# A weight sum tied behind splits of activations, and one head's outputs stored in two parts

## The chip, the cores and the metric

The kernel runs on one core of one Trainium2 chip. The metric is the time of one execution on the device in microseconds, as the median of several runs.

## The reference

The computation is one inference step of a two-layer trunk for 512 sample tokens and 128 prompt tokens, 2048 channels, float32. Each layer takes an RMS norm with shift and scale from a conditioning vector, one wide input projection whose columns feed two mixers and their gates, one output projection, and a gated residual. The second layer's first mixer is differential attention with four heads. Cut to that and to what follows it:

```python
cq, ck, cv, cg, dq, dk, dv, dg = split_cols(h @ w_in, ODD_SPLIT)
...
o1 = attend(cq[:, 0][:, :, None], ck_all[:, 0], cv_all)[:, :, 0]
o2 = attend(cq[:, 1][:, :, None], ck_all[:, 1], cv_all)[:, :, 0]
o_c = rms_norm(o1 - lam.astype(o1.dtype) * o2, c_on) * (1.0 - lam_init)
y_c = o_c.transpose(0, 2, 1, 3).reshape(b, t, C_W) * jax.nn.silu(cg)
y_d = merge_heads(attend(q_d, dk_all, dv_all)) * jax.nn.silu(dg)
return jnp.concatenate([y_c, y_d], axis=-1) @ w_out, new
...
xp = xp + gt_p * out_p
xs = xs + gt_s * out_s
```

`x_prompt` and `x_sample` give the two groups of tokens; both go through the same weights.

## The kernel before

All 640 tokens lie side by side on the free axis: columns 0 to 511 are the sample, 512 to 639 (`SPLIT`) the prompt; a half is 320 columns (`HALF`, `HV`). Channels lie on the 128 partitions, so an activation of 2048 channels is 16 tiles `h0` to `h15`. Matrix products keep float32 accuracy by splitting each operand into a high and a low part: ScalarE copies the high part (`split`, line 328), VectorE subtracts it (line 329), and TensorE makes three products (lines 364 to 366, and 667 to 669 in pairs of tiles). Weights come in quarters of 256 KB (`load_raw`, line 341, tile `raw`, four buffers) or in halves of 512 KB (`load8`, line 582, tile `w8`, shown as `w`, four buffers).

The instructions of each engine run in a fixed order. That order is not the order of the code: the framework plans it before the run from its own estimates of durations, taking what it thinks is ready first, and earlier code before later code among that. An engine that waits for an instruction's input holds everything behind it. The same holds for the loads that SyncE (SP) issues and the stores that GpSimd (POOL) issues.

**The last output projection** (`project`, `project_out`, called with layer 1) takes the 16 output tiles in three kinds. Tiles 0 to 3 and the first steps of the next work run while the last attention ends. Tiles 4 and 5 are made singly; the last single tile, 5, makes all its second halves of columns first (PSUM `pb`) and then the first halves (`pa`). From tile 6 on, tiles come in pairs by seven half-sized products M1 to M7 in place of eight (Strassen's scheme with Winograd's sums, `run_pairs`). For that, sums and differences of the activations' quarters are needed:

- `forms` makes them during the single tiles, for j = 0 to 7 from the tiles j and j + 8: three forms x2, x3, x4 in a tile `x` (lines 1284 to 1286), which is split into the tiles `T`, and a difference `d` = b12 - b11 (line 1287), kept unsplit in `t1[j]`. The inputs `ya`, `yb` come from DRAM into two `w8` buffers. `x` lies in the tile `sx` (one buffer). `d` lies in the free places `tables` for j < 4, in `sf` for j = 4 to 6, and for j = 7 over b11 itself in its `w8` buffer.
- When tile 5 has read the second halves of h0 to h7, `project` writes the split differences over them (lines 328 and 329, `h<-tables`, `h<-sf`, `h<-w`). They are the moving operand of M5.
- `run_pairs` loads the weight blocks A11, A21, A22 (two quarters in `raw`) and A12. The operand of M5 is the sum A21 + A22, made in two instructions (line 606) in a tile `sx`, the same buffer as the forms' x. M6 and M3 change that sum in place (lines 609, 618); line 611 makes another difference in `sf`. All these are split before use. M1 takes A11 as it is.

Results of a tile are added to the residual (`res_sum`, line 1304, tile `xr`), turned by TensorE (line 697), copied and stored (`rows_out`). A fill of VectorE work (lines 211 and 213, weights of the modulation in `adaw` and `tables`, loaded by POOL, line 218) runs beside it.

**The differential heads** (`diff_gen`) work in units of 128 query tokens: units 0 to 3 are the sample, 4 the prompt. Unit u is scored in step u (lines 927 to 929, maxima in line 889, exponentials in line 896), weighed two steps later (lines 1733 to 1738, a norm with POOL's lines 1743 and 1744 and VectorE's line 1748), and turned and written to `y` by `out` another step later (lines 1753 to 1758). Heads 0, 1 and 3 have their gates ready, and `out` multiplies with them. The third head, h = 2, has none (`gt is None`); its two output tiles y4 and y5 are copied by ScalarE (line 1756) and stored by POOL to DRAM (`save_y`, line 1050, `ydram`). Their gates are the last two tiles of the input projection (columns `cg` 4 and 5, `last_gate`, `very_late_gate`): the head's output is loaded again (line 1413, tile `yg`), the gate is made from PSUM (lines 1415 and 1416), the product (line 1419, tile `gg`) goes to DRAM (line 1420), and `y1_maker` (line 2046) loads it for the output projection.

Of the kernel before, what the change touches and what calls it, by code (L numbers as in the profile page):

```python
# [23 lines left out]
NS = 512  # L24
NP = 128
NT = NS + NP
HALF = NT // 2
# [5 lines left out]
SPLIT = slice(NS, NT)  # L33
# [21 lines left out]
def trunk_kernel(ctx: ExitStack, tc: tile.TileContext, I: dict, O: dict):  # L55
    nc = tc.nc
    V, A, PE, G = nc.vector, nc.scalar, nc.tensor, nc.gpsimd
# [31 lines left out]
    def psT():  # L89
        return pT.tile([P, 512], F32, tag="T", name="T")  # L90
# [236 lines left out]
    def split(hi, lo, x):  # L327
        A.activation(hi, x, AF.Copy)  # L328
        V.tensor_sub(lo, x, hi)  # L329
# [46 lines left out]
    prep, attn = [], []  # L376
# [12 lines left out]
    late = []  # L389
# [648 lines left out]
    ydram = [dram.tile([P, NT], F32, name=f"yd{k}") for k in range(KT)]  # L1038
# [6 lines left out]
    y = [None] * KT  # L1045
    st = {"sets": 1, "rp": 3}

    def save_y(*ks):
        for k in ks:
            nc.gpsimd.dma_start(ydram[k], y[k])  # L1050
# [198 lines left out]
    def big(tag, shape=(P, NT), dtype=F32, bufs=1):  # L1249

        n = 6 * HALF if tag[0] == "T" else 8 * P
        return pools["cur"].tile([P, n], dtype, tag=tag, name=tag, bufs=bufs)

    def forms(src):

        f = None

        kept = isinstance(src, dict)

        def load(j):  # L1260
            if kept:
                return src[j], src[j + 8]
            if src is None:
                for k, n in ((j, "acc"), (j + 8, "sq")):
                    V.tensor_add(st[n], *hs[k])
                return st["acc"], st["sq"]
            ts = [big("w8", bufs=4)[:, 0:NT] for _ in range(2)]
            for i in range(2):
                nc.sync.dma_start(ts[i], src[j + 8 * i])
            return ts  # L1270

        T.clear()
        t1.clear()
        nxt = load(0) if src and not kept else None
        for j in range(8):
            (ya, yb), nxt = nxt or load(j), (load(j + 1) if src and not kept and j < 7 else None)
            b11, b12, b21, b22 = ya[:, 0:HALF], ya[:, HALF:NT], yb[:, 0:HALF], yb[:, HALF:NT]
            x = big("sx")[:, 0:3 * HALF]
            if f is None:
                f = big("sf")  # L1280
            d = (room[j] if j < 4 else f[:, (j - 4) * HALF:(j - 3) * HALF] if j < 7
                 else big("w8", bufs=4)[:, 0:HALF] if kept else b11)
            x2, x3, x4 = (x[:, i * HALF:(i + 1) * HALF] for i in range(3))
            V.tensor_sub(x3, b22, b12)
            V.tensor_add(x2, b11, x3)
            V.tensor_sub(x4, b21, x2)
            V.tensor_sub(d, b12, b11)
            t = big(f"T{FORM_AT[j] if kept else j}", dtype=F32R).rearrange("p (s n) -> p s n", s=2)
            split(t[:, 0, :], t[:, 1, :], x)
            T.append(t)  # L1290
            t1.append(d)
            yield
# [113 lines left out]
        project(W_OUT[l], [n * P for n in range(KT)], n0, maker, job, begin, done, tail, **kw)  # L1406


    def very_late_gate(i, places):
        def f(pp):  # L1410
            ap = pools["cur"]
            ti, t, g = (ap.tile([P, NT], F32, tag=tag, name=n, bufs=b) for n, (tag, b) in zip(("yg", "gt_t", "gg"), places))
            nc.sync.dma_start(ti, ydram[i])
            for j, sl in HV:
                A.activation(t[:, sl], pp[j][:, 0:HALF], AF.Tanh, scale=0.5)
                V.scalar_tensor_tensor(out=g[:, sl], in0=t[:, sl], scalar=1.0, in1=pp[j][:, 0:HALF],
                                       op0=ALU.add, op1=ALU.mult)
            yield
            V.tensor_mul(g, ti, g)
            nc.gpsimd.dma_start(ydram[i], g)  # L1420
        return f

# [269 lines left out]
    def diff_gen(ap, h, v, kq):  # L1692

        gt = gates_back(2 * h)
        t = y_pair(2 * h) if gt is None else gt
        ps, pts, ons, rls, fins, rns = {}, {}, {}, {}, {}, {}

        maps = []

        def score(u, m):  # L1700
            segs, masks, lo, hi, _ = blk_plan(u, False)
            n = hi - lo
            k, q = kq[m]
            s = scores(q, u, k, segs)
            maps.append(soft(ap, 768, s[:, lo:hi], n, q[2][u]))
            if m == 0:
                return
            pp, ll, _ = zip(*maps)
            maps.clear()
            ps[u] = pp[0]  # L1710

            def mix():
                rr = [inverse(l) for l in ll]
                w = small.tile([P, 1], F32, tag="w", name="w")
                V.scalar_tensor_tensor(out=w, in0=ll[0], scalar=nlam, in1=rr[1], op0=ALU.mult, op1=ALU.mult)
                V.scalar_tensor_tensor(out=pp[0][:, 0:n], in0=pp[1][:, 0:n], scalar=w, in1=pp[0][:, 0:n],
                                       op0=ALU.mult, op1=ALU.add)
                rls[u] = rr[0]
            fins[u] = later_on(mix)

        def groups(u):
            n = len(blk_plan(u, False)[4])
            fins.pop(u)()
            pts[u] = [pt_group(ap, [ps[u][:, i * P:(i + 1) * P] for i in range(c0, min(c0 + 4, n))])
                      for c0 in range(0, n, 4)]

        def weigh(u):
            chunks = blk_plan(u, False)[4]
            last = len(chunks) - 1
            o = psT()[:, 0:256]  # L1730
            pieces = [(i, c, [x[:, (i % 4) * P:(i % 4) * P + P] for x in pts[u][i // 4]]) for i, c in enumerate(chunks)]
            for i, c, (ph, _) in pieces:
                PE.matmul(o, ph, v[0][:, c, :], start=(i == 0), stop=False)
                PE.matmul(o, ph, v[1][:, c, :], start=False, stop=False)
            for i, c, (_, pl) in pieces:
                PE.matmul(o, pl, v[0][:, c, :], start=False, stop=(i == last))
            on = ap.tile([P, 256], F32, tag="on", name="on", bufs=2)
            A.activation(on, o, AF.Copy, scale=rls[u])
            both = small.tile([P, 2], F32, tag="ssq", name="ssq")
            ssq, rns[u] = both[:, 0:1], both[:, 1:2]  # L1740
            junk = ap.tile([P, 256], BF16, tag="junk", name="junk")
            A.activation(junk, on, AF.Square, accum_out=ssq)
            G.tensor_scalar(ssq, ssq, 1.0 / 256, EPS, ALU.mult, ALU.add)
            G.tensor_tensor(rns[u], ssq, half[:, 0:1], op=ALU.pow)
            ons[u] = on

        def norm(u):
            V.scalar_tensor_tensor(out=ons[u], in0=ons[u], scalar=rns[u], in1=st["con"], op0=ALU.mult, op1=ALU.mult)

        def out(u):  # L1750
            x = psT()
            for j in range(2):
                PE.transpose(x[:, j * P:(j + 1) * P], ons[u][:, j * P:(j + 1) * P], ident)
            d, x = t[:, :, u * P:(u + 1) * P], x[:, 0:256].rearrange("p (j q) -> p j q", j=2)
            if gt is None:
                A.copy(d, x)
            else:
                V.tensor_mul(d, x, d)

        yield  # L1760
        for u in range(8):
            if u >= 3:
                out(u - 3)
            if 2 <= u < 7:
                weigh(u - 2)
            if u < 5:
                score(u, 0)
            if u == 7:
                break
            yield  # L1770
            if u >= 2:
                norm(u - 2)
            if u < 5:
                score(u, 1)
            if u == 4:
                passed["scores"] += 1
            if u == 6:
                passed["values"] += 1
            if 1 <= u < 6:
                groups(u - 1)  # L1780
            yield
        save_y(2 * h, 2 * h + 1)
        passed["heads"] += 1


# [162 lines left out]
    def gates_back(i):  # L1948
        if i not in FRONT:
            return None  # L1950
        t = y_pair(i)
        for j in range(2):
            nc.sync.dma_start(t[:, j, :], gdram[i + j])
        return t
# [65 lines left out]
        jobs.append((OD["cq"] + h * P, q_job("q0", "c_q_norm", keep=("x2", 1))))  # L2020
        jobs.append((OD["cq"] + (4 + h) * P, with_rest("q1", "c_q_norm", head_rest, h, done0 + 4 + h)))
    def last_gate(i):
        late = very_late_gate(i, (("rp", 3), ("stg", 2), ("rp", 3)))

        def f(pp):
            wait_for("heads", 3)
            return late(pp)
        return f
# [20 lines left out]
    def last_pool():  # L2049
        close("odd")  # L2050
        close_psum("twice")
        open_psum("more")
        open_pool("fin")
        for n in range(2):
            res_load(1, n)
        attn.append(forms(ydram))

    def rows_out(n):
        xr = st["xr", n]
# [94 lines left out]
```

## Time and profile before

| | us |
|---|---|
| median of three runs | 2225.78 |
| the three runs | 2224.23, 2225.78, 2227.52 |
| the profiled execution | 2222.26 |
| its span, first to last instruction | 2220.5 |
| busy in it: TensorE matmuls | 2189.8 |
| VectorE | 1741.9 |
| ScalarE | 1128.7 |
| GpSimd | 251.5 |

Rows of a timeline give the start from the beginning of the span and the duration in microseconds, engine, line, operation, out<-in with shapes, and how often; a bracket gives how long the engine stood idle before it and what ended that. "SPq" is SyncE's queue of loads. Rows of waits give the sum, the number and the longest. Rows of transfers give their number, the size of one in KB and the median time from issue to landing.

### The profile page before, as it was taken

Reading aid. Unit: us, or ns where it says so; the run is one execution under the profiler, and the core shown is the slowest. Engines: PE = TensorE matmul, PEld = TensorE weight load, DVE = VectorE, ACT = ScalarE, POOL = GpSimd, SP = SyncE. Lnnn points to the kernel's source line nnn. Section 1 sums busy time; section 2 is a strip of 40 time slices with the busy share of each in tenths; the row PEclk is TensorE's granted clock in tenths of the full one; section 3 lists DMA queues with packets and bytes.
Section 4 is the critical chain, followed back from the end, with each engine's and each line's share of the span. In section 5 each row is a group of like instructions: output and inputs, shape, how many; then the busy total and the mean of one; then the engine's idle time right before and its main releaser. Section 6 shows DMA issues by size and latency. Waiting matters only on the chain.

```text
span 2220.5 us, 40890 instructions
## 1 busy us (share of the span) xinstructions
PE 2189.8 (99%) x15456; PEld 2121.2 (96%) x15456; DVE 1741.9 (78%) x3047; ACT 1128.7 (51%) x2405; POOL 251.5 (11%) x401
## 2 busy tenths in 40 slices
PE   7999999999999999999999999999999999999999
PEld 5899999999999999999999999999999999989998
DVE  5669898989888977877888878978667666677775
ACT  4335453535334445444644466554577766663343
POOL 3220000000100100000101012211010011111110
PEclk9999999999999999999999999999999999999999
DMA  9986556565554435844554434545523233347641
GB/s 367 336 295 185 174 160 207 178 199 159 158 151 123 146 100 185 248 137 125 168 153 142 145 98 128 167 140 163 176 81 97 68 115 112 117 128 256 194 141 52
DMA packets 377172, 359.26 MB, mean 162 GB/s; under 512 B 18562, under 2 KB 326240, under 8 KB 376464
## 3 DMA queue, kind: packets, MB, share of 16 engines
q1 hardware_dynamic: 354944, 279.54, 41.6%
q0 software_dynamic: 21168, 74.90, 9.6%
q8 instruction: 121, 1.98, 0.4%
q10 hardware_dynamic: 864, 2.23, 0.3%
q14 instruction: 75, 0.61, 0.1%
HBM read 307.17 MB, written 44.17 MB: 158 GB/s over the span
## 4 chain that ended last, share of the span: by engine, by line
PE 90%; DMA 4%; DVE 3%; issue 2%; ACT 1%; POOL 0%; SPq 0%; DVEq 0%; POOLq 0%; ACTq 0%
PE pq L667 13%; PE pq L669 12%; PE pq L668 12%; PE pa L364 6%; PE pa L365 6%; PE pb L364 6%; PE pa L366 6%; PE pb L366 6%; PE pb L365 6%; PE T L915 2%; PE S L927 1%; PE S L928 1%; PE T L195 1%; PE S L929 1%; PE T L978 1%
## 5 line engine op out<-in xcount | busy, mean ns | idle before, releaser
L328 ACT ACTIVATE wh<-raw 128x512 fp32r<-128x512 f32 (+1 forms) x352 | 210.5, 600 | 316.2 <-PE pb L365 194.0
L667 PE MATMUL pq<-h,wh 128*128 128x320 f32 x1152 | 359.0, 312 | 0.0
L669 PE MATMUL pq<-h,wl 128*128 128x320 f32 x1152 | 356.5, 309 | 0.0
L668 PE MATMUL pq<-h,wh 128*128 128x320 f32 x1152 | 356.4, 309 | 0.0
L364 PE MATMUL pa<-h,wh 128*128 128x320 f32 x944 | 299.2, 317 | 1.0 <-ACT h L328 1.0
L364 PE MATMUL pb<-h,wh 128*128 128x320 f32 x944 | 295.9, 314 | 0.0
L365 PE MATMUL pa<-h,wh 128*128 128x320 f32 x944 | 294.5, 312 | 0.0
L366 PE MATMUL pb<-h,wl 128*128 128x320 f32 x944 | 294.1, 312 | 0.0
L365 PE MATMUL pb<-h,wh 128*128 128x320 f32 x944 | 293.7, 311 | 0.0
L366 PE MATMUL pa<-h,wl 128*128 128x320 f32 x944 | 292.9, 310 | 0.0
L329 DVE TENSOR_TENSOR wl<-raw,wh 128x512 fp32r<-128x512 f32 (+1 forms) x352 | 228.7, 650 | 76.4 <-ACT wh L328 72.1
L667 PE MATMUL pq<-T,wh 128*128 128x320 f32 x864 | 269.0, 311 | 0.4 <-DVE tables L646 0.4
L669 PE MATMUL pq<-T,wl 128*128 128x320 f32 x864 | 267.3, 309 | 0.4 <-DVE wl L329 0.4
L668 PE MATMUL pq<-T,wh 128*128 128x320 f32 x864 | 267.2, 309 | 0.0
L328 ACT ACTIVATE wh<-sx 128x512 fp32r<-128x512 f32 x216 | 135.7, 632 | 181.9 <-PE pq L668 111.9
L667 PEld LDWEIGHTS pq<-h,wh 128*128 128x128 f32 x1152 | 216.4, 188 | 2.1 <-issue 2.1
L668 PEld LDWEIGHTS pq<-h,wh 128*128 128x128 f32 x1152 | 216.5, 188 | 0.0
L669 PEld LDWEIGHTS pq<-h,wl 128*128 128x128 f32 x1152 | 216.3, 188 | 0.0
L282 DVE SCALAR_TENSOR_TENSOR acc<-adaw,sT,acc 128x1024 f32<-128x1024 f32 x150 | 189.2, 1277 | 0.0
L364 PEld LDWEIGHTS pa<-h,wh 128*128 128x128 f32 x944 | 177.3, 188 | 11.1 <-issue 8.7
L365 PEld LDWEIGHTS pa<-h,wh 128*128 128x128 f32 x944 | 177.6, 188 | 5.0 <-issue 4.7
L329 DVE TENSOR_TENSOR wl<-sx,wh 128x512 fp32r<-128x512 f32 x216 | 147.8, 688 | 43.4 <-ACT wh L328 39.7
(438 smaller groups left out, 4949.6 us busy)
## 6 DMA issues: line engine op xcount, KB each, us to landing
adaw<-in_ada_w SPq DMA_DIRECT2D x80, 512.0 KB, 4.2
raw<-in_ev_w_in SPq DMA_DIRECT2D x130, 256.0 KB, 3.6
raw<-in_od_w_in SPq DMA_DIRECT2D x112, 256.0 KB, 3.0
w<-in_od_w_in SPq DMA_DIRECT2D x48, 512.0 KB, 4.2
ada<-in_ada_w SPq DMA_DIRECT2D x11, 2048.0 KB, 13.1
adaw<-in_ada_w POOLq DMA_DIRECT2D x69, 256.0 KB, 3.6
w<-in_ev_w_in SPq DMA_DIRECT2D x27, 512.0 KB, 3.8
adah<-in_ada_w SPq DMA_DIRECT2D x20, 512.0 KB, 9.0
```

The lines of the kernel that those rows point to most:

```text
L195: PE.matmul(acc[32 * g:32 * g + 32, 0:wd], sT[:, kt, :], w[:, kt % m, :], start=(i < 4), stop=(i >= KT - 4), tile_position=(0, 32 * g))
L282: V.scalar_tensor_tensor(out=acc[c], in0=w, scalar=sT[:, kt, c:c + 1], in1=acc[c], op0=ALU.mult, op1=ALU.add)
L328: A.activation(hi, x, AF.Copy)
L329: V.tensor_sub(lo, x, hi)
L364: PE.matmul(ps, wh[:, i, :], hi[:, sl], start=(j == js[0] if alone else (pos == 0 and j == 0)), stop=False)
L365: PE.matmul(ps, wh[:, i, :], lo[:, sl], start=False, stop=False)
L366: PE.matmul(ps, wl[:, i, :], hi[:, sl], start=False, stop=(j == js[1] - 1 if alone else (pos == 3 and j == 3)))
L667: PE.matmul(ps, wh[:, j, :], hi, start=(first and h == 0 and j == 0), stop=False, skip_group_check=True)
L668: PE.matmul(ps, wh[:, j, :], lo, start=False, stop=False, skip_group_check=True)
L669: PE.matmul(ps, wl[:, j, :], hi, start=False, stop=(final and h == 1 and j == 3), skip_group_check=True)
L915: PE.transpose(t[:, i * P:(i + 1) * P], p, ident)
L927: PE.matmul(d, q[0][:, bs], k[0][:, ks], start=True, stop=False)
```

## The change

Two independent edits.

In the forms of the last projection alone (`hold`), for j = 7: the tile `x` with the forms lies in a `w8` buffer instead of `sx`, and the difference `d` lies in `sx` instead of over b11. The tile `sx` is thus held until that difference has been split over h7, and the sums of line 606, which need the same buffer, come after that split.

For the third differential head: instead of two stores of 640 columns behind the last unit, there are two stores of the 512 sample columns after unit 3 is written (step 6) and two of the 128 prompt columns after unit 4 (step 7). The two late gates of these tiles load the two parts separately and multiply them separately; the product is stored in one piece as before.

```diff
-    def forms(src):
+    def forms(src, hold=False):
...
-            x = big("sx")[:, 0:3 * HALF]
+            x = (big("w8", bufs=4) if hold and j == 7 else big("sx"))[:, 0:3 * HALF]
             if f is None:
                 f = big("sf")
             d = (room[j] if j < 4 else f[:, (j - 4) * HALF:(j - 3) * HALF] if j < 7
-                 else big("w8", bufs=4)[:, 0:HALF] if kept else b11)
+                 else big("sx")[:, 0:HALF] if hold else big("w8", bufs=4)[:, 0:HALF] if kept else b11)
...
-    def very_late_gate(i, places):
+    def very_late_gate(i, places, parts=(slice(0, NT),)):
...
-            nc.sync.dma_start(ti, ydram[i])
+            for sl in parts:
+                nc.sync.dma_start(ti[:, sl], ydram[i][:, sl])
...
-            V.tensor_mul(g, ti, g)
+            for sl in parts:
+                V.tensor_mul(g[:, sl], ti[:, sl], g[:, sl])
             nc.gpsimd.dma_start(ydram[i], g)
...
             if u >= 3:
                 out(u - 3)
+            if gt is None and u >= 6:
+                for k in (2 * h, 2 * h + 1):
+                    sl = SPLIT if u == 7 else slice(0, NS)
+                    nc.gpsimd.dma_start(ydram[k][:, sl], y[k][:, sl])
...
-        save_y(2 * h, 2 * h + 1)
+        if gt is not None:
+            save_y(2 * h, 2 * h + 1)
...
-        late = very_late_gate(i, (("rp", 3), ("stg", 2), ("rp", 3)))
+        late = very_late_gate(i, (("rp", 3), ("stg", 2), ("rp", 3)), (slice(0, NS), SPLIT))
...
-        attn.append(forms(ydram))
+        attn.append(forms(ydram, True))
```

## Prediction

> **What bounds the kernel now.** The page first: TensorE is busy all but 30.7 us of the span, so only time in which TensorE stands or runs slowly can be won.
>
> ```profile
> span 2220.5 us, 40890 instructions
> PE 2189.8 (99%) x15456; PEld 2121.2 (96%) x15456; DVE 1741.9 (78%) x3047; ACT 1128.7 (51%) x2405; POOL 251.5 (11%) x401
> ```
>
> The profiled execution took 2222.26 us, 1.76 more than its span; the median of the three runs is 2225.78, which is 3.52 above the profiled one. I work out a difference on the profiled run and take it off the median. A measurement of this kernel can tell about 0.2%, 4.45 us, from no change.
>
> Then the waits of TensorE over the whole span, longest first. The first belongs to the start of the kernel; the next two lie where the change acts.
>
> ```profile
> PE T L1078 <- DMA xb<-in_x_sample: 6.5, 2, 5.1
> PE T L697 <- issue: 2.8, 1, 2.8
> PE S L927 <- ACT p L896: 2.4, 1, 2.4
> ```
>
> **The place of the tie.** Four stretches around the second of these waits (columns: length, busy time of PE, PEld, DVE, ACT and POOL, then granted clock, DMA share, GB/s):
>
> ```profile
> 2065.00:2069.00 4.00, 3.87 (x25) 3.34 (x23) 1.30 (x2) 3.73 (x9) 0.00 (x0) 1.00 0.22 64
> 2069.00:2072.00 3.00, 0.33 (x3) 0.26 (x3) 2.19 (x5) 0.41 (x1) 0.00 (x0) 1.00 0.08 24
> 2072.00:2076.00 4.00, 4.00 (x18) 3.88 (x18) 4.00 (x11) 0.75 (x2) 1.35 (x3) 0.57 0.72 216
> 2076.00:2080.00 4.00, 4.00 (x30) 4.00 (x29) 3.00 (x4) 0.63 (x1) 0.47 (x1) 1.00 0.82 241
> ```
>
> TensorE loses 0.13 + 2.67 us standing and then, at a granted clock of 0.57, another 4.00 x 0.43 = 1.72 us. The timelines of VectorE and of TensorE say why:
>
> ```profile
> 2059.64 0.68 DVE L329 TENSOR_TENSOR wl<-raw,wh 128x512 fp32r<-128x512 f32 x1
> 2065.82 0.69 DVE L606 TENSOR_TENSOR sx<-w,raw 128x512 f32<-128x512 f32 x1 [5.49 <-DMA raw<-in_od_w_out]
> ...
> 2069.81 0.69 DVE L606 TENSOR_TENSOR sx<-w,raw 128x512 f32<-128x512 f32 x1 [2.69 <-DMA raw<-in_od_w_out]
> ...
> 2071.02 0.55 DVE L1304 SCALAR_TENSOR_TENSOR xr<-pa,hgt,xr 128x320 f32<-128x320 f32 x1
> 2071.48 0.67 DVE L1304 SCALAR_TENSOR_TENSOR xr<-pb,hgt,xr 128x192 f32<-128x192 f32 x2
> ...
> 2072.67 1.69 DVE L329 TENSOR_TENSOR h<-tables,h 128x320 fp32r<-128x320 f32 x4
> ...
> 2075.48 0.49 DVE L329 TENSOR_TENSOR h<-w,h 128x320 fp32r<-128x320 f32 x1
> 2071.67 1.07 PE L697 MATMUL T<-ident,xr 128*128 128x128 f32 x5 [2.77 <-issue]
> 2084.51 0.31 PE L667 MATMUL pq<-h,wh 128*128 128x320 f32 x1
> ```
>
> VectorE reaches the two sums of L606 (A21 + A22, the operand of M5) before their weights have landed, and holds 5.49 + 2.69 us for them. Behind them in its queue stand the residual sum of tile 4 (L1304), which the transposes of L697 need: the first starts 0.1 us after the first L1304 has written. Yet the sums themselves are not urgent. M1 begins at 2084.51 and has 24 matmuls, at 30 in 4.00 us some 3.2 us, so M5 begins near 2087.7.
>
> **Part one, the tie: what it moves.** The sums write the tile "sx". Before, it came free when the last form's x had been split; now the last difference lies in it, so the sums cannot run before the split h<-w (2075.48 here). VectorE has nothing else to wait for in 2060 to 2069: the splits wl and the three pieces of L1304 run when their inputs are there, and the eight splits of differences follow. TensorE's 0.13 + 2.67 us go, and with the pause the slow stretch, 1.72: 4.5 us. The sums cost nothing at their new place as long as they are covered by what is left of tile 5 and by M1: they must have begun by 2087.7 - 4.5 (the shift) - 0.68 (split wl) - 0.68 (its high part, taken as long) - 0.69 = 2081.1. Even at the old times the last split is done at 2076.0, so the cover is 5 us.
>
> What else the edit moves is one slot of "w8". The last x now takes one of the four, so the loads of A11, A21 and A12 each get the slot that came free one step later:
>
> ```profile
> 2057.41 0.48 DVE L1287 TENSOR_TENSOR w<-w 128x320 f32<-128x320 f32 x1
> 2052.31 1.45 SPq L582 DMA_DIRECT2D w<-in_od_w_out  x2
> 2057.52 0.37 SPq L582 DMA_DIRECT2D w<-in_od_w_out  x1
> 2058.52 2.20 SPq L341 DMA_DIRECT2D raw<-in_od_w_out  x2
> raw<-in_od_w_out SPq DMA_DIRECT2D x1, 256.0 KB, 5.4
> ```
>
> Two 512 KB loads (A11, A21) left at 2052.31, A12 at 2057.52 when L1286 and L1287 let go. Now A21 leaves with A12 near 2057.8, and the raw weights behind it on SP near 2058.9, with 0.5 MB more in front of them. The raw load of 2058.52 (tile 5's last quarter) took 5.4 us to land; at the 241 GB/s of the stretch above, 0.5 MB more is 2.1 us, so it lands near 2066.4. TensorE uses it after the transposes (2071.67 - 2.77 + 0.7) and one more quarter (12 matmuls, 1.6), near 2071.2, and its two splits (0.68 each) come before; so some 3 us of cover hide it, and without them each us late is one of TensorE. The next pair's A11, which used to wait for the last difference (the same split), now finds the x slot free from 2060 on. It is needed 25 us later. Nothing here is priced above zero; the bounds of part one are 0 and 4.5, and I take 4.5, since the wait and its releaser are both seen.
>
> **Part two, the third head's outputs.** The third of TensorE's waits:
>
> ```profile
> 1952.03 0.95 DVE L889 TENSOR_REDUCE nm<-S 128x1 f32<-128x768 f32 x1
> 1957.22 0.83 DVE L1419 TENSOR_TENSOR gg<-yg,gg 128x640 f32<-128x640 f32 x1 [4.24 <-DMA yg<-yd]
> 1957.96 0.15 DVE L907 RECIPROCAL rl<-l 128x1 f32<-128x1 f32 x1
> 1960.95 0.45 PE L927 MATMUL S<-k1h,q1h 128*128 128x384 f32 x1 [2.42 <-ACT p L896]
> ```
>
> VectorE holds 4.24 us for the gate's copy of head output y4, the maxima (L889) of the fourth head stand behind it, and TensorE stands 2.42 us for the exponentials made from them. The way of y4 through DRAM:
>
> ```profile
> 1942.91 0.37 ACT L1756 COPY y<-T 128x256 f32<-128x256 f32 x1 [0.72 <-PE T L1753]
> 1941.98 2.63 POOL L853 TENSOR_TENSOR rq<-rq,half 128x12 f32<-128x12 f32 x1 [1.63 <-ACT rq L851]
> 1944.99 0.29 POOL L1743 TENSOR_SCALAR ssq<-ssq 128x1 f32<-128x1 f32 x1 [0.39 <-ACT junk L1742]
> 1945.95 0.49 DVE L1748 SCALAR_TENSOR_TENSOR on<-on,ssq,con 128x256 f32<-128x256 f32 x1 [0.71 <-POOL ssq L1744]
> 1947.05 0.38 PE L1753 MATMUL T<-ident,on 128*128 128x128 f32 x2
> 1948.73 1.16 POOL L1050 DMA_DIRECT2D yd<-y  x2 [2.82 <-ACT y L1756]
> 1953.79 0.34 SPq L1413 DMA_DIRECT2D yg<-yd  x1
> yd<-y POOLq DMA_DIRECT2D x2, 320.0 KB, 5.2
> yg<-yd SPq DMA_DIRECT2D x2, 320.0 KB, 4.2
> out_y_prompt<-ot POOLq DMA_DIRECT2D x15, 64.0 KB, 3.2
> qsw<-qd SPq DMA_DIRECT2D x16, 64.0 KB, 2.7
> 1940.79 0.28 DVE L329 TENSOR_TENSOR ptl<-T,pth 128x128 fp32r<-128x128 f32 x1
> 1973.14 0.42 DVE L1758 TENSOR_TENSOR y<-T,y 128x256 f32<-128x256 f32 x1 [0.20 <-PE T L1753]
> ```
>
> The four sample blocks are complete with the copy of 1942.91. Their two stores (256 KB each) go to POOL's queue when L853 ends, 1944.6, take 1.16 us as the two of L1050 did, and push ssq (L1743) from 1944.99 to 1945.8. Behind ssq wait L1748 (1945.95 to about 1946.8) and the transposes of the prompt block, so TensorE may stand 0.2 us at L1753, which runs at 1947.05 today. The sample parts then land near 1950 (5.2 for a larger store) and their load near 1954.5 at the latest (4.2), so the prompt part is the one that is late: stored at 1948.9, landing after 3.2 (a 64 KB store) to 5.2, loaded in 2.7 (a 64 KB load) to 4.2. So it is there between 1954.8 and 1958.3. These transfers share the stretch with a weight load and the sample loads, so I take values between, 4.0 and 3.0: 1955.9. The prompt part of the product costs 0.28, and L907 starts near 1956.3 instead of 1957.96, 1.7 us earlier. TensorE's 2.42 shrinks by 1.7, less the 0.2: 1.5 us won, with ends of 2.2 won (the whole wait) and 0.8 lost.
>
> What this part adds elsewhere is covered. The product of each gate becomes two, 0.68 + 0.28 for 0.83, and SP issues two loads more, while it stands 4 us for the store anyway. The fourth head's gates (L1953) and a weight load queue behind them on SP, and are first used at 1973.14.
>
> **Sum:** 4.5 + 1.5 = 6.0 us; 2225.78 - 6.0 = 2219.8 (the profiled run 2216.3).
>
> **Rivals.**
> The store split brings nothing: the prompt part's own round trip ends as late as the whole one did (5.2 + 4.2), and the delay on POOL costs 0.2 to 0.8. For it: those are the rows of this very place. Against it: they are of transfers five times as large, two of them at once. 4.5 - 0.5 = 4.0 us, 2221.8.
>
> The slow clock is not the pause's doing. The low clock stands right behind a pause of 2.77 us, yet a pause of 2.42 (1958.5) left the clock at full and, at the start, one of 5.1 shows none either. If the slow stretch comes anyway, part one wins 2.8 alone: 2.8 + 1.5 = 4.3, 2221.5. The Trainium skill, "TensorE: Matmul & The Clock Gate", Part 1, has the clock halved after an idle window of about 3.4 us that runs free of the kernel; read strictly a pause of 2.77 us is too short for it, and by that rule the 4.3 would hold. The trace has 0.57 directly behind the pause and 1.00 before it, so I side with the trace.
>
> The change doesn't do what it says: another instruction that is late takes the place of the sums in VectorE's queue, or the two parts of a row of the DRAM tile are ordered against each other as one, so that both loads wait for the prompt store. Nothing in this trace shows a tile in DRAM that is written in two parts and read in two. Part one not acting gives about 0 to 1.5 won: 2225.
>
> Slower: the wait moves to M5. Tied behind the splits, the sums stand where the rows of the modulation fill also wait for their loads; if the planner puts several of those ahead, M5's weights are late. It costs from a start of the sums at 2081.1 on, us for us, and from 2.8 us on the slow clock again. To undo 6.0 and lose 4.45 more, less 1.7 for the clock, the sums must start near 2090. Against it: the sums stand before the fill's rows in the code, and 2090 is 14 us behind the last split. 2230.5.
>
> **How the numbers follow.** Forecast 0.55; no gain from the stores 0.20; slow clock anyway 0.08; not as said 0.10; wait at M5 0.07. Faster by over 0.2% is most of the forecast (0.52 of 0.55, since 6.0 stands 1.5 above the bound) and 0.11 from the two rivals that end at the bound: 0.63. Slower is 0.07, the rest, 0.30, within 0.2%. The range: upward it takes in the change that does nothing, 2226.0; downward it takes the whole of TensorE's 2.42 and the 1.6 by which the lowest of three runs lies under the median: 2225.78 - 4.5 - 2.4 - 1.6 = 2217.3, and a little for the short waits after 1960 that follow from the same backlog on VectorE: 2216.0.
>
> **What would show it.** Right: no L606 on VectorE before the split h<-w, L697 without a wait, a granted clock of 1.00 from tile 5 to M1. For part two: two stores near 1944.6, a hold before the second product under 3 us, the wait at L927 under 1 us. Wrong: a wait at L667 of M5 for sx, a wait for tile 5's raw weights, L927 waiting as long as before, or the slow clock without a pause ahead of it.

## The result, and the profile after

| | before | after |
|---|---|---|
| median, first comparison (18 runs each) | 2224.06 us | 2220.09 us |
| lowest and highest | 2220.97, 2228.11 | 2217.29, 2225.47 |
| ratio of the times, 95% interval | | 0.9982 [0.9975, 0.9989] |
| profiled execution | 2222.26 | 2222.19 |

The change wins 0.18% of 2224, 4.0 us, with an interval of 2.4 to 5.6. Two later comparisons of the same two kernels gave 0.9977 [0.9968, 0.9986] and 0.9986 [0.9977, 0.9995], 5.1 and 3.1 us. What is "won", here and below, is one minus the ratio, times the median of before in that comparison. The profiled execution of after is one of its slower ones and equals that of before; so the two spans by themselves show nothing, and the stretches have to be read one by one. Lines from 1413 on have moved: L1753 is now L1755, L1419 is L1421, and so on.

The page of after, and its waits of TensorE over the whole span:

```profile
span 2220.4 us, 40909 instructions
PE 2192.6 (99%) x15456; PEld 2123.5 (96%) x15456; DVE 1742.6 (78%) x3049; ACT 1129.0 (51%) x2405; POOL 252.3 (11%) x403
```

```profile
PE T L697 <- DVE m L743: 2.0, 1, 2.0
...
PE T L697 <- issue: 1.5, 1, 1.5
...
PE T L697 <- ACT ot L2068: 1.0, 1, 1.0
```

The wait at L927 is off the list, and so is the one of 2.8 at L697. But two others at L697 have come, 1.5 and 1.0. They do not belong to tile 4. The stretches (columns as in the prediction: length, busy time of PE, PEld, DVE, ACT and POOL, granted clock, DMA share, GB/s) put them a tile earlier, at the transposes of tile 3:

```profile
2056.00:2060.00 4.00, 1.77 (x12) 1.19 (x10) 4.00 (x9) 2.65 (x5) 0.00 (x0) 1.00 0.98 284
2060.00:2064.00 4.00, 3.80 (x17) 3.83 (x18) 1.86 (x4) 0.35 (x2) 1.29 (x2) 0.63 1.09 327
2064.00:2068.00 4.00, 4.00 (x27) 4.00 (x27) 1.24 (x2) 0.63 (x1) 0.00 (x0) 0.95 1.10 367
2068.00:2072.00 4.00, 4.00 (x30) 4.00 (x29) 2.88 (x8) 2.98 (x7) 0.00 (x0) 1.00 0.43 128
```

TensorE stands 2.23 + 0.20 us there, and a slow clock follows (0.63 and 0.95: 4.00 x (0.37 + 0.05) = 1.68 us). From 2068 on, where before had its pause, it runs through. The timeline of after there, all VectorE but for the transposes (L697) of tile 3 and, at 2072.44, of tile 4:

```profile
2052.45 0.75 DVE L213 SCALAR_TENSOR_TENSOR adaS<-adaw,sT,adaS 128x512 f32<-128x512 f32 x1 [3.10 <-DMA adaw<-in_ada_w]
...
2054.58 0.48 DVE L1284 TENSOR_TENSOR w<-w,w 128x320 f32<-128x320 f32 x1
...
2057.46 0.48 DVE L1287 TENSOR_TENSOR sx<-w 128x320 f32<-128x320 f32 x1
2057.86 0.55 DVE L1304 SCALAR_TENSOR_TENSOR xr<-pa,hgt,xr 128x320 f32<-128x320 f32 x1
...
2058.51 0.72 PE L697 MATMUL T<-ident,xr 128*128 128x128 f32 x4 [1.45 <-issue]
2058.65 1.15 DVE L329 TENSOR_TENSOR T<-w,T 128x960 fp32r<-128x960 f32 x1
2059.71 0.35 DVE L1304 SCALAR_TENSOR_TENSOR xr<-pb,hgt,xr 128x128 f32<-128x128 f32 x1
2060.20 0.30 PE L697 MATMUL T<-ident,xr 128*128 128x128 f32 x1 [0.98 <-ACT ot L2068]
...
2072.44 0.71 PE L697 MATMUL T<-ident,xr 128*128 128x128 f32 x5
...
2073.14 0.49 DVE L329 TENSOR_TENSOR h<-sx,h 128x320 fp32r<-128x320 f32 x1
...
2074.68 1.29 DVE L606 TENSOR_TENSOR sx<-w,raw 128x512 f32<-128x512 f32 x2
```

The tie does what it says: the two sums (L606) run behind the split h<-sx, without a hold, and tile 4's transposes do not wait. But the last form (L1284 to L1287, and its split T<-w between the pieces of L1304) now stands in front of tile 3's residual sum. The brackets of L697 name other releasers, but the times point to that sum: four transposes start 0.10 us after its first piece has ended (2057.86 + 0.55), the fifth 0.14 us after its last (2059.71 + 0.35). In before the two stood the other way round:

```profile
2053.86 0.54 DVE L1304 SCALAR_TENSOR_TENSOR xr<-pa,hgt,xr 128x320 f32<-128x320 f32 x1
...
2055.61 0.49 DVE L1284 TENSOR_TENSOR sx<-w,w 128x320 f32<-128x320 f32 x1
```

Before, the last x had to wait until the form ahead of it had left "sx". With a buffer of its own it is ready early, and the planner takes it early. By this reading it would cost little if VectorE were on time, but the fill's row (L213) has held it for 3.10 us just before; the experiments test both halves of that.

The third head's outputs in after, first the timelines of POOL and VectorE, then the transfers from issue to landing:

```profile
1947.20 1.16 POOL L1769 DMA_DIRECT2D yd<-y  x2
1948.43 0.19 POOL L1745 TENSOR_SCALAR ssq<-ssq 128x1 f32<-128x1 f32 x1
...
1950.98 1.15 POOL L1769 DMA_DIRECT2D yd<-y  x2 [1.72 <-ACT y L1758]
...
1954.60 0.69 DVE L1421 TENSOR_TENSOR gg<-yg,gg 128x512 f32<-128x512 f32 x1
1955.21 0.95 DVE L889 TENSOR_REDUCE nm<-S 128x1 f32<-128x768 f32 x1
1957.39 0.29 DVE L1421 TENSOR_TENSOR gg<-yg,gg 128x128 f32<-128x128 f32 x1 [1.23 <-DMA yg<-yd]
```

```profile
yd<-y POOLq DMA_DIRECT2D x2, 256.0 KB, 2.7
yg<-yd SPq DMA_DIRECT2D x2, 256.0 KB, 3.6
yd<-y POOLq DMA_DIRECT2D x2, 64.0 KB, 1.9
yg<-yd SPq DMA_DIRECT2D x2, 64.0 KB, 3.7
```

This execution is 2.6 us later at this place than before's for reasons ahead of the change (below), so 1947.20 answers to the forecast 1944.6. ssq is pushed, as forecast, and a hold of 1.23 is left of 4.24.

**A ledger by stretches.** Three matmuls that come in every kernel in the same order cut the span into four stretches: A, the last score matmul on `k0h` (L927) with 256 columns ahead of the third head's stores; M, the last transposes of L1753, at the end of the fourth head; B, the first matmul of M1. In before A and M are

```profile
1926.11 0.36 PE L927 MATMUL S<-k0h,q0h 128*128 128x256 f32 x1
2002.67 0.38 PE L1753 MATMUL T<-ident,on 128*128 128x128 f32 x2
```

and B is the L667 of 2084.51 in the prediction. In after the three are

```profile
1928.75 0.36 PE L927 MATMUL S<-k0h,q0h 128*128 128x256 f32 x1
2002.23 0.38 PE L1755 MATMUL T<-ident,on 128*128 128x128 f32 x2
2083.55 0.31 PE L667 MATMUL pq<-h,wh 128*128 128x320 f32 x1
```

A to M holds part two, M to B part one. The same differences of all profiled executions, experiments included (us):

| kernel | start to A | A to M | M to B | B to end |
|---|---|---|---|---|
| before | 1926.1 | 76.6 | 81.8 | 136.0 |
| stores_only | 1930.7 | 73.4 | 78.3 | 138.3 |
| tie_only | 1927.4 | 75.2 | 78.4 | 135.5 |
| clean_tie_alone | 1927.0 | 75.5 | 76.9 | 135.7 |
| after; after_same_chip; after_third | 1928.8; 1930.6; 1928.6 | 73.5; 73.3; 73.8 | 81.3; 78.3; 78.8 | 136.9; 136.5; 136.4 |
| clean_tie; clean_tie_again | 1927.7; 1930.7 | 73.9; 74.0 | 76.9; 76.9 | 136.5; 136.2 |
| fill_later; fill_later_again | 1930.6; 1927.9 | 73.1; 73.8 | 76.9; 76.9 | 136.8; 136.9 |
| clean_fill | 1928.5 | 73.4 | 76.9 | 136.8 |
| before_fill | 1929.4 | 75.4 | 76.9 | 141.3 |

For the profiled pair: + 2.6 - 3.1 - 0.5 + 0.9 = - 0.1. The 2.6 lies in code that the change does not touch; 1.7 of it is a slow clock behind a wait for L743 (last section).

### The profile page after: what moved, and what is told of

It reads as the page before. It is cut to its first block, busy times and chain, and to the rows that moved or that the text cites. A ratio compares the mean times of both kernels' runs of the same rounds, so it can differ in the third digit from the quotient of the medians.

```text
span 2220.4 us, 40909 instructions
## 1 busy us (share of the span) xinstructions
PE 2192.6 (99%) x15456; PEld 2123.5 (96%) x15456; DVE 1742.6 (78%) x3049; ACT 1129.0 (51%) x2405; POOL 252.3 (11%) x403
## 3 DMA queue, kind: packets, MB, share of 16 engines
q10 hardware_dynamic: 864, 2.23, 0.3%
## 5 line engine op out<-in xcount | busy, mean ns | idle before, releaser
L667 PE MATMUL pq<-h,wh 128*128 128x320 f32 x1152 | 358.7, 311 | 0.0
L329 DVE TENSOR_TENSOR wl<-raw,wh 128x512 fp32r<-128x512 f32 (+1 forms) x352 | 228.5, 650 | 78.3 <-ACT wh L328 74.7
L667 PE MATMUL pq<-T,wh 128*128 128x320 f32 x864 | 268.8, 311 | 0.4 <-DVE tables L646 0.4
L667 PEld LDWEIGHTS pq<-h,wh 128*128 128x128 f32 x1152 | 216.4, 188 | 2.1 <-issue 2.1
```

What stands on the lines that cost most here:

```text
L667: PE.matmul(ps, wh[:, j, :], hi, start=(first and h == 0 and j == 0), stop=False, skip_group_check=True)
```

## The experiments

The name of each is that of the ledger. All were timed in five rounds against before on the same chip; the median of before was 2224.11 on the first chip (the first four), 2223.43 on the second (before_fill, clean_fill, after_same_chip) and 2222.84 on the third (the rest). The difference of the medians themselves is not always what the ratio gives: it is 1.4 us more in stores_only, 1.1 more in clean_tie, 0.6 less in after_same_chip, and within 0.7 in the others.

**tie_only**: part one alone; stores and loads as before.

```diff
-            if gt is None and u >= 6:
-                for k in (2 * h, 2 * h + 1):
-                    sl = SPLIT if u == 7 else slice(0, NS)
-                    nc.gpsimd.dma_start(ydram[k][:, sl], y[k][:, sl])
...
-        if gt is not None:
-            save_y(2 * h, 2 * h + 1)
+        save_y(2 * h, 2 * h + 1)
...
-        late = very_late_gate(i, (("rp", 3), ("stg", 2), ("rp", 3)), (slice(0, NS), SPLIT))
+        late = very_late_gate(i, (("rp", 3), ("stg", 2), ("rp", 3)))
```

> The tie alone, as the change makes it; the third head's stores are as before. Theory A (the last form's own buffer lets its instructions be planned ahead of tile 3's residual sum, so one pause replaces another): no pause of over 1 us at the transposes of tile 4, but a pause of 2 to 2.5 us at those of tile 3, with a slow stretch of up to 1.7 us in some runs; the wait of 2.4 us of the fourth head's scores stays. Time 0 to 2.5 us below the kernel before. Theory B (the pause at tile 3 comes from a late load that the profiled run happened to have): no pause at tile 3, 4 to 5 us below.

2220.40 us, 0.9985 [0.9976, 0.9993]: 3.3 won. The timeline of TensorE has, at L927 and at tile 3,

```profile
1961.24 0.45 PE L927 MATMUL S<-k1h,q1h 128*128 128x384 f32 x1 [1.36 <-ACT p L896]
...
2059.17 0.30 PE L697 MATMUL T<-ident,xr 128*128 128x128 f32 x1 [0.98 <-ACT ot L2063]
```

The new wait at tile 3 comes with the tie, not with the stores. Here it is 0.98 for the fifth transpose alone and leaves the clock at full; theory A had the place right, but expected a pause of at least 2. The time lies between the two theories, and the wait at L927 is 1.4 here, where before's profile had 2.4.

**stores_only**: part two alone; the last form as before.

```diff
-        attn.append(forms(ydram, True))
+        attn.append(forms(ydram))
```

> The stores in two parts alone, no tie. Theory A: the wait of 2.4 us of the fourth head's scores is gone, the pause of 2.8 us at tile 4's transposes stays: 2 to 2.6 us below the kernel before. Theory B (all of the measured gain is the tie's): 0 to 0.5 us below.

2220.97 us, 0.9992 [0.9982, 1.0001]: 1.8 won, with an interval that just touches none. No wait at L927. The sums still hold VectorE, but the pause behind them is 1.0 and brings no slow clock:

```profile
2064.84 0.69 DVE L606 TENSOR_TENSOR sx<-w,raw 128x512 f32<-128x512 f32 x1 [3.44 <-DMA raw<-in_od_w_out]
...
2069.22 0.69 DVE L606 TENSOR_TENSOR sx<-w,raw 128x512 f32<-128x512 f32 x1 [3.09 <-DMA raw<-in_od_w_out]
...
2071.09 0.93 PE L697 MATMUL T<-ident,xr 128*128 128x128 f32 x5 [1.03 <-ACT h L328]
```

So the pause that part one removes is not always the 2.8 + 1.7 of the first profile: M to B is 78.3 here, 81.8 there, with the same code and the same order on VectorE. But what is short in M to B is in part paid behind B, where this profile needs 138.3 and before's 136.0. VectorE and TensorE there:

```profile
2083.33 1.55 DVE L213 SCALAR_TENSOR_TENSOR adaS<-tables,sT,adaS 128x512 f32<-128x512 f32 x2 [1.83 <-DMA tables<-in_ada_w]
2084.79 0.68 DVE L329 TENSOR_TENSOR wl<-w,wh 128x512 fp32r<-128x512 f32 x1
2085.53 0.41 PE L669 MATMUL pq<-h,wl 128*128 128x320 f32 x1 [0.90 <-DVE wl L329]
```

A row of the fill waits for its load, a split of M1 stands behind it, and TensorE waits 0.9, then 0.7 more for a residual sum (L697): 1.6 of the 2.3. In before the same row comes at 2083.44, but B comes 2.1 us later than here, and TensorE waits for neither. From M to the end of the span stores_only needs 78.3 + 138.3 = 216.6; clean_tie and clean_tie_again (below, with the same stores) need 213.4 and 213.1 by the same sum.

**clean_tie**: the whole change, but the last x stays in "sx", and when it is split a second tile "sx" takes the difference. The sums are tied as in after; no "w8" buffer is used, and the last form cannot be pulled ahead.

```diff
-            x = (big("w8", bufs=4) if hold and j == 7 else big("sx"))[:, 0:3 * HALF]
+            x = big("sx")[:, 0:3 * HALF]
...
-            V.tensor_sub(d, b12, b11)
+            if not last:
+                V.tensor_sub(d, b12, b11)
...
+            if last:
+                d = big("sx")[:, 0:HALF]
+                V.tensor_sub(d, b12, b11)
```

> Both edits, but the last form's x stays in the buffer sx, and only after its split is the last difference written there: the tie holds, and the last forms stay behind the ones before them. Theory A: no pause of over 1 us in 2040 to 2080, sums behind the splits; 2.8 + 1.7 + 2.4, so 6 to 7 us below the kernel before and 2 to 4 below the changed one. Theory B: the pause at tile 3 depends on the load, so as the changed kernel, about 4 us below.

2217.63 us, 0.9976 [0.9966, 0.9986]: 5.3 won. In its timeline the first of tile 3's sums (here L1309) ran at 2052.78, ahead of the last form, and the sums of L606 behind the split (h<-sx):

```profile
2068.09 0.49 DVE L329 TENSOR_TENSOR h<-sx,h 128x320 fp32r<-128x320 f32 x1
...
2069.63 1.29 DVE L606 TENSOR_TENSOR sx<-w,raw 128x512 f32<-128x512 f32 x2
```

TensorE waits for nothing at tile 3 or 4; M to B is 76.9.

**fill_later**: the whole change, with the fill's rows two tiles later.

```diff
-                lead_pp=(0, 2), fill=fill2, fill_at=4, rests=fin_rests)
+                lead_pp=(0, 2), fill=fill2, fill_at=6, rests=fin_rests)
```

> The changed kernel, with the modulation fill starting at the pairs instead of at tile 4, so that VectorE does not hold 3.1 us for a fill row's load among the single tiles. Theory A: the order alone makes some pause, but without the hold VectorE comes to tile 3's residual sum in time: pause under 1 us, 5 to 7 us below the kernel before, less what the fill's rows cost later (eight rows of 0.75 us move to the fourth pair, where VectorE has to finish them: up to 3 us). If the hold plays no part the pause stays at 2.4 us and the time at 4 us below or less.

2217.57 us, 0.9972 [0.9962, 0.9982]: 6.2 won. The last form is still in front of tile 3's sum, yet that sum is early, since no row of the fill has held VectorE:

```profile
2052.92 0.48 DVE L1287 TENSOR_TENSOR sx<-w 128x320 f32<-128x320 f32 x1
...
2053.92 0.54 DVE L1304 SCALAR_TENSOR_TENSOR xr<-pa,hgt,xr 128x320 f32<-128x320 f32 x1
```

M to B is 76.9 again. The last x lies in a "w8" buffer here as in after, so the weight loads that go one slot later are not what makes TensorE wait at tile 3. Two causes are needed for the new wait, the order and the fill's rows; taking either away removes it. That it is the hold of these rows, and not only their place, is not separated: without them the planner also puts the split T<-w ahead of all pieces of the sum.

**before_fill**: the same edit to the fill, in the kernel before.

> The kernel before, with one edit: the modulation fill's rows on VectorE begin two tiles later (fill_at 6 in place of 4). No part of the change is in it; the two sums of L606 still stand ahead of tile 4's residual sum. Theory A (the sums hold VectorE for their own weights): tile 4's L697 still waits 1 to 3 us, by when the raw weights land, and the time is within 1 us of before, 2223 to 2225. Theory B (the fill's loads and holds are what makes VectorE late there, also before): the sums' holds and the wait at tile 4 go, and the time falls by 3 to 4.5, to 2220 to 2221. The wait at L927 stays in both, 1.4 to 2.4 us.

2222.17 us, 0.9996 [0.9988, 1.0005]: 0.9 won, not told from none. That is the time of theory A, but not for its reason: the pause at tile 4 is gone (M to B 76.9), as theory B had it, although the sums still hold VectorE: their weights land earlier. The loads of `raw` issued between 2050 and 2066 took a median of 2.8 us here and 5.4 in before, and the fill's load (256 KB) that before has in that stretch is missing here; whether it is that load or the earlier issue that makes the difference was not tested. But behind B 5.3 us are lost (136.0, 141.3). The timeline of VectorE, the longest of TensorE's waits behind 2110, and the slow stretch:

```profile
2062.08 0.69 DVE L606 TENSOR_TENSOR sx<-w,raw 128x512 f32<-128x512 f32 x1 [2.94 <-issue]
...
2066.14 0.69 DVE L606 TENSOR_TENSOR sx<-w,raw 128x512 f32<-128x512 f32 x1 [2.77 <-DMA raw<-in_od_w_out]
...
2127.68 0.76 DVE L213 SCALAR_TENSOR_TENSOR adaS<-tables,sT,adaS 128x512 f32<-128x512 f32 x1 [3.21 <-DMA tables<-in_ada_w]
...
2129.48 0.68 DVE L329 TENSOR_TENSOR wl<-sx,wh 128x512 fp32r<-128x512 f32 x1
```

```profile
PE pq L669 <- DVE wl L329: 2.7, 1, 2.7
```

```profile
2132.00:2136.00 4.00, 4.00 (x22) 4.00 (x21) 4.00 (x9) 1.26 (x2) 0.00 (x0) 0.69 0.43 127
```

A row of the fill waits 3.21 us for its load, a split that TensorE needs stands behind it, TensorE waits 2.7, and a slow clock follows. It is the same kind of pause with another row in front, as behind B in stores_only.

**clean_fill**: the clean tie and the later fill together.

> The tie without a w8 buffer for the last form (the difference is made in sx after the x there has been split), the outputs stored in two parts, and the fill two tiles later. Each of the two edits by itself removed the wait at tile 3 that the change brought (5.3 and 6.2 us won in all). Theory A (both took the same 2 us away): together no more than either, 5.5 to 6.5 won, 2217.6 to 2218.6, and no wait over 0.5 us of TensorE between 2040 and 2110. Theory B (they remove different stalls, the fill also a contention of transfers): the gains add, 7 to 8 won, 2216 to 2217.

2218.12 us, 0.9979 [0.9970, 0.9987]: 4.7 won, less than either theory had, M to B 76.9. The gains do not add, as theory A had it: both edits took the same wait away.

**after_same_chip**: the changed kernel on that chip.

> The changed kernel again, on the chip of the two others. Theory A: 3.5 to 4.5 us under before as in the first comparison, with TensorE waiting 1 to 3 us in all at L697 of tile 3. Theory B: the same time; this run only gives the yardstick for the others.

2218.94 us, 0.9977 [0.9968, 0.9986]: 5.1 won. Its new wait is 1.0 at full clock, M to B 78.3. clean_fill's median is 0.8 lower, though by the ratios it won less (4.7 against 5.1).

**after_third, clean_tie_again, fill_later_again, clean_tie_alone** share the third chip. The last one is the kernel before with the clean tie alone (the edits of clean_tie and tie_only together).

> The changed kernel, as the yardstick of the three others on one chip. Both theories: 4 to 5 us under before.

2219.42 us, 0.9986 [0.9977, 0.9995]: 3.1 won, less than both theories had. The waits at tile 3 are 1.0 and 0.5, at full clock.

> The tie made without a w8 buffer, and the outputs in two parts, now on the same chip as the changed kernel. Theory A (the wait at tile 3 that the change brought is paid in nearly every run, 1 to 2.4 us, and sometimes a slow clock behind it): 1 to 2.5 us under the changed kernel's median. Theory B (the wait is hidden by later slack, or is an accident of the first profiles): the same as the changed kernel within 0.7 us.

2218.53 us, 0.9982 [0.9973, 0.9991]: 4.0 won, 0.9 under after_third's median.

> The changed kernel with the modulation fill two tiles later, on the same chip. Theory A: 1 to 2.5 us under the changed kernel's median, as with the clean tie. Theory B: the same as the changed kernel within 0.7 us.

2218.07 us, 0.9981 [0.9972, 0.9990]: 4.2 won, 1.35 under. Both lie at the edge between the theories: that the new wait costs something is shown by M to B (78.3 to 81.3 in the three profiles of the change, 76.9 in the five without the wait); that the time falls by its 1 us or so when it goes is not settled. The medians fall in all three comparisons (0.8, 0.9, 1.35), but the intervals of the ratios overlap in each, and in the first of the three the ratios have it the other way.

> The clean tie without the stores in two parts: part one of the change as it was priced, 4.5 us won. Theory A (the price was right, the last form's buffer spoiled it): 4 to 5 us under before in the median, no wait of TensorE at L697 over 0.5 us, the wait at L927 there still with 1.3 to 2.4. Theory B (tile 4's pause costs less in the usual run, since its length hangs on the landing of the weights): 2 to 3.3 us, no more than the tie with the changed last form, which won 3.3.

2218.89 us, 0.9983 [0.9975, 0.9992]: 3.8 won, between the theories. No wait at L697 over 0.2 and M to B at 76.9; the wait at L927 is there, and the hold of VectorE that it comes from:

```profile
PE S L927 <- ACT p L896: 1.8, 1, 1.8
```

```profile
1957.43 0.83 DVE L1426 TENSOR_TENSOR gg<-yg,gg 128x640 f32<-128x640 f32 x1 [3.59 <-DMA yg<-yd]
```

The fastest versions are clean_tie, fill_later and clean_fill, 4.0 to 6.2 us under before; by their intervals they cannot be told from each other, nor from the changed kernel.

## Why the prediction was right in its number, and where it was not

Forecast were 2219.8 us and a gain of 6.0; measured 2220.09 and 4.0, 5.1 and 3.1 in three comparisons. The number came out nearly right because the runs of before in the comparison had a median of 2224.06 and not the 2225.78 from which the 6.0 was taken off. That is luck. The forecast gain was 1 to 3 us too large, and 0.18% (0.23 and 0.14 in the others) lies at the bound of 0.2% that the prediction set, not clearly beyond it.

**The tie acts as told.** No L606 in front of the splits, L697 of tile 4 without a wait, a clock of 1.00 from 2068 on; the cover held (the sums begin at 2074.68, and neither M5 nor tile 5's weights were waited for), so the rival with the wait at M5 fell.

**The step that failed** is the sentence on the slot of "w8", "Nothing here is priced above zero". It followed the slot to the loads behind it and asked what comes late; it did not ask what comes early. The last form, freed from "sx", went in front of tile 3's residual sum, and with the fill's rows and their hold (1.2 to 3.1 us in the four profiles that have both) TensorE now stands 1.0 to 2.5 us there, once with a slow clock of 1.7 behind it. clean_tie and fill_later, which each take one of the two causes away, run M to B in 76.9. In the ledger that is 1.4 to 4.4 us of part one lost again; the medians with and without it differ by about one. The rival that another late instruction takes the place of the sums on VectorE came nearest, but it had part one not acting at all.

**Part one's 4.5 was sized from one profile.** M to B was 81.8 in before's, 5.0 above the unbroken 76.9, close to the priced 4.5. But stores_only, with the same order there, needs 78.3. So within M to B the pause costs from 1.4 to 5.0 us by run; counted from M to the end, with what stores_only loses behind B, it is 3.2 to 3.5 there (216.6 against 213.4 and 213.1) and 5.2 in before (217.8 against the 212.6 of clean_tie_alone). A clean tie alone won 3.8, and its interval, 1.8 to 5.6, does not exclude 4.5. The size was about right, then, but the profile gave one draw, the one with the slow clock, and the term should have been a mean over runs.

**Part two was worth more in the traces than its price; the times cannot tell.** The term 1.5 stood on a prompt round trip of 4.0 + 3.0; the store landed in 1.9 and the load took 3.7, and the hold shrank to 1.23, so the whole wait of 2.42 went. A to M is 75.2 to 76.6 in the four profiles with whole stores and 73.1 to 74.0 in the nine with stores in two parts: means 75.6 and 73.6, 2.1 won. But the 2.42 was the longest of its kind: in the four profiles with whole stores the wait at L927 is 2.4, 1.4, 1.8 and 1.3, and it is in none of the nine others. The rival that the stores bring nothing fell in the trace. In the times they show less: 1.8 alone, and on the third chip 4.0 with and 3.8 without them, a difference that the intervals cannot resolve. Some of it may be given back at the end: the eight profiles with both parts need 136.2 to 136.9 from B on, the three with whole stores and the early fill 135.5 to 136.0. A wait of 0.4 for the residual at a later L697 is half of that; where the rest comes from was not found. (stores_only, at 138.3, is a case of its own, see there.)

**The slow clock.** As forecast, it goes with the pause where the pause goes: from M to B the clock is full in every profile where TensorE stands less than 2 us there, and falls in the two where it stands longer (before and after). Every slow place in the thirteen profiles lies behind a pause; that a given pause brings one is not so (last section). The rival that it would come anyway is false for tile 4.

## What to carry to other kernels

Giving a tile another buffer does not only free or block loads: it changes when its instructions are ready, and a planner that takes what is ready may put them in front of something. So ask of every removed dependency what may now come early, and which short-lived work behind it has no slack. Price a pause of TensorE as a range with and without the slow clock behind it, from several profiles where they can be had, and hold one stretch against the same stretch of another kernel, cut at matmuls that both have, where the spans are noisy. Read the stretches behind it too: what one stretch wins the next may lose, as in stores_only.

## What the runs showed of the hardware that was not expected

**The same pause may or may not halve the clock.** Early in the kernel, in code that no experiment touched, TensorE waits about 2 us for a maximum (L743). The stretch behind it, in after, in clean_tie and in fill_later:

```profile
172.00:176.00 4.00, 3.79 (x19) 3.80 (x20) 4.00 (x9) 3.24 (x9) 0.00 (x0) 0.68 0.50 150
```

```profile
172.00:176.00 4.00, 3.50 (x25) 3.50 (x26) 4.00 (x8) 3.24 (x9) 0.00 (x0) 1.00 0.57 179
```

```profile
176.00:180.00 4.00, 4.00 (x20) 4.00 (x19) 4.00 (x8) 1.95 (x6) 0.00 (x0) 0.62 0.66 185
```

The waits there were 2.0, 2.0 and 2.3. Over the thirteen profiles the clock fell behind six of these waits (2.0 to 2.3) and stayed at full behind seven (1.8 to 2.1), while a pause of 2.42 at L927 in before left it at full. Cut into stretches of 2 us, and without the last 9 us of the span, the thirteen profiles have eleven slow places: these six, tile 4 in before, tile 3 in after, 32 us in fill_later (behind a wait of 3.2), 2130 in before_fill (behind 2.7), and 760 in stores_only, behind waits of 0.95 and 0.65 with two matmuls between them. Each costs 1.7 us (1.66 to 1.72 by the granted clock of its stretches, which goes down to 0.50), about as much as the change wins in one of its parts. It goes with the spread from run to run: of the 40 runs of after, the 7 with a mean clock of 0.998 or less took 2222.7 us in the mean, the other 33 took 2219.1. The Trainium skill, "TensorE: Matmul & The Clock Gate", Part 1, has the clock fall after an idle window of about 3.4 us whose phase runs free of the kernel. That equal pauses differ agrees with a free phase. The pauses of 2.0 us, and the 0.95 and 0.65 in stores_only, are shorter than that window, so by these traces it need not be idle from end to end.

**The two parts of the head's outputs landed sooner than the whole, but not by size alone.** In after the stores of 64 KB took 1.9 us and those of 256 KB 2.7 (1.8 to 1.9 and 2.4 to 2.7 in the nine profiles with parts), where the two of 320 KB in before took 5.2. The loads of 256 and of 64 KB took 3.6 and 3.7, no less for the smaller. Yet a store of 64 KB to `out_y_prompt`, issued at 2061.08 in before, took 5.8. The Trainium skill, "DMA: Bandwidth & Descriptors", "Anatomy of one DMA", fits a transfer issued by GpSimd by 2.0 us and its bytes at 436 GB/s, which gives an estimate of 2.2 and 2.6 for the stores of the two parts; these agree within 0.3, while the 5.2 and the 5.8 do not.
